# One sum of a seven-product weight scheme moved from VectorE to an accumulating DMA, and steps at five places of a decoder layer moved

## The chip, the core and the metric

The kernel runs on one core of a Trainium2 chip. It is one launch; the time is device microseconds of the program. TensorE (PE) does matmuls and transposes, VectorE (DVE), ScalarE (ACT) and GpSimd (POOL) do the rest, SyncE (SP) and GpSimd issue DMAs. Times of before: 1010.71, 1011.93 and 1009.23 us, median 1010.71.

## The reference, cut to what matters

One decoder layer, batch 1, 256 tokens, width 2048, all in float32. One input projection feeds four causal mixers of 4 heads of 128; each mixer's output is gated, projected, weighted by a sigmoid gate and summed; then the output projection, the residual and a last RMS norm.

```python
h = rms_norm(x, norm_w)
p = h @ w_in                                   # 256 x 2048 times 2048 x N_IN
(z, gate, dsa_qkv, idx_q, idx_k, idx_w, fox_qkv, fox_f, diff_qkv, dil_qkv) = split(p)
branches = (dsa(...), fox(...), diff(...), dilated(...))     # top-k, forgetting, differential, dilated
for b in range(4):
    y = branches[b] * silu(z[b])
    term = sigmoid(gate[b]) * (y @ w_branch[b])
    merged = term if b == 0 else merged + term
return rms_norm(x + merged @ w_out, final_norm_w)
```

In the first mixer an indexer scores all keys for each query (16 small heads) and keeps the best 64, so its attention can start only when that selection is made.

## The kernel before, in words

Every float32 operand is split in two: `hi`, a rounded copy that ACT writes (`split_hi`, line 193), and `lo`, the rest, that DVE writes as raw minus hi (`split_lo`, line 206). A product of one 128-row block is three matmuls (lines 362 to 364: hi with hi, hi with lo, lo with hi).

Most weight columns are done in groups of 1024 output columns by 2048 rows. One half of the rows is done plainly: the four *c* units c2a, c2b, c1a, c1b, of 24 matmuls each. The other half is a 2 by 2 block product done with seven block products instead of eight (`seven`, line 432): units u1 to u7 of 12 matmuls each. They need sums of weight blocks B11, B12, B21, B22, each 128 partitions by 2048 numbers, 1 MB, in raw slots 0, 1, 3 and 2. `plus` (line 173) makes such a sum on DVE in place: B12+=B11 (u5), B12+=B22 (u6), B11=B12-B11 (u7), B21+=B12 (u4). They also need sums of the activations, made once for each source, `asum`, split into the tile `sf` (lines 420 to 429). There are 16 such groups of w_in, four for each branch (qk, zv, and two of the gate, here gate group 1 and 2), and a 17th, the *late* group, for columns of w_out at the end. Products gather in four PSUM banks X, Y, Z, W; between products ACT and DVE read a bank before the next product writes it (lines 526 to 565). Of the `read`s in `seven`, that of u7 is line 530 on ACT, that of Z by c2b lines 534 and 554.

The order is one list of units. For unit i the loop at the end of the program emits `low` (the lo split of the half five halves ahead), `high` (the hi split seven halves ahead; at a unit's second half also the `pre` sums of the unit two further), the unit's matmuls, its `post` reads, perhaps one step of the running threads, then `begin` (the start of new threads). Eight hi and six lo half buffers, shared in turn, hold the splits, so a split waits for the matmuls that used its buffer before. A slot is filled anew when `free` is called on it; SP's queue issues these loads in order. GpSimd's queue issues the DMAs of the merge buffers `md` and `mp`, of bias tables, and of x for the residual.

Everything that is not a weight product is a thread, a generator: the norm of x (`rms_thread`, which writes `rp`), the indexer and top-k with the gate logarithms (`ps_ix`, lines 726 to 750; `cps`, lines 664 to 669; `lf`), heads (`lps`, `ptp`, `o`, and for the differential mixer `od` and `otd`), merges (`mtp`, lines 908 to 921). At each `yield` a thread gives way. A step of all threads is run each time that the costs of the units since the last one reach 20; a product costs 12, any other unit 24. A unit with a `need` first drains the threads that it names.

The loop and the threads' pace:

```python
for h in range(2):
    low(2 * i + h + LO - 1)
    high(2 * i + h + HI - 1)
    u.mm(u, h)
for f in u.post:
    f()
since += u.cost
if since >= PACE:
    since = 0
    run_threads()
begin(u)
```

## Time and profile before

| what | value |
| --- | --- |
| median of three runs | 1010.71 us (1009.23 to 1011.93) |
| profiled execution | 1009.36 us |
| its span | 1007.7 us |
| busy PE, DVE, ACT, POOL | 958.3, 856.1, 630.1, 47.5 us |
| mean granted clock of TensorE | 0.977 |
| DMA | 195.81 MB, mean 194 GB/s |

The span is the time from the first instruction to the last in the profiled execution; the rest of its time lies around it. Busy shares are means over stages: PE is busy 95% of the span, and what is left is seen best in its list of waits. A wait names who waited, for what, and how long. The granted clock is a share of full speed; in a window with a low value every matmul takes longer.

### The profile page before, as it was taken

How to read it: one execution, taken by the hardware profiler on the slowest of the kernel's cores; microseconds unless marked ns; L12 is line 12 of the kernel's file. 1: busy time of each engine (PE TensorE's matmuls, PEld its weight loads, DVE VectorE, ACT ScalarE, POOL GpSimd, SP SyncE). 2: the span in 40 equal slices, each digit the busy share in tenths (PEclk: the TensorE clock that was granted, in tenths of full speed). 3: DMA queues.
4: the chain of work that ended last, by engine and by line, in shares of the span. 5: the costliest groups of instructions: out<-in, count | busy, mean ns of one | idle time of the engine just before them, and what ended most of it. 6: DMA issues, size and time to landing. Idle time of an engine off the chain costs nothing.

```text
span 1007.7 us, 12090 instructions
## 1 busy us (share of the span) xinstructions
PE 958.3 (95%) x4443; PEld 793.4 (79%) x4443; DVE 856.1 (85%) x1016; ACT 630.1 (63%) x809; POOL 47.5 (5%) x67
## 2 busy tenths in 40 slices
PE   9979996999999999999999999979999999985996
PEld 8857885778888888888888877868888888873786
DVE  5689999999898989987997998968898998499762
ACT  5756853697655667974566778745556796353541
POOL 2010000000000000000100000101000000100130
PEclk9999999899999999999999999989999999987999
DMA  9926463455767556468857464648755645931702
GB/s 319 295 90 222 139 212 122 168 167 204 264 220 238 180 170 235 173 201 260 233 173 246 170 202 132 213 164 207 257 182 173 220 174 201 392 135 42 264 29 84
DMA packets 100043, 195.81 MB, mean 194 GB/s; under 512 B 7811, under 2 KB 10021, under 8 KB 99600
## 3 DMA queue, kind: packets, MB, share of 16 engines
q1 hardware_dynamic: 96240, 181.06, 52.8%
q0 software_dynamic: 3712, 13.98, 5.3%
q8 instruction: 35, 0.57, 0.2%
q14 instruction: 24, 0.20, 0.1%
q10 hardware_dynamic: 32, 0.01, 0.0%
HBM read 186.61 MB, written 8.41 MB: 194 GB/s over the span
## 4 chain that ended last, share of the span: by engine, by line
PE 81%; DVE 10%; issue 3%; ACT 3%; DMA 2%; POOL 0%; ACTq 0%; POOLq 0%; DVEq 0%
PE ps_g L362 10%; PE ps_g L363 10%; PE ps_g L364 10%; PE ps_zv L362 5%; PE ps_zv L364 5%; PE ps_zv L363 5%; PE ps_qk L364 5%; PE ps_qk L362 5%; PE ps_qk L363 5%; DVE wlo L206 4%; PE ps_o L363 2%; PE ps_b L362 2%; PE ps_b L363 2%; PE ps_b L364 2%; PE ps_o L362 2%
## 5 line engine op out<-in xcount | busy, mean ns | idle before, releaser
L193 ACT ACTIVATE whi<-raw 128x1024 fp32r<-128x1024 f32 (+1 forms) x439 | 444.6, 1051 | 231.2 <-DVE raw L173 93.3
L206 DVE TENSOR_TENSOR wlo<-raw,whi 128x1024 fp32r<-128x1024 f32 (+1 forms) x439 | 519.0, 1218 | 52.5 <-ACT whi L193 19.1
L173 DVE TENSOR_TENSOR raw<-raw 128x2048 f32<-128x2048 f32 x68 | 155.6, 2288 | 30.8 <-DMA raw<-in_w_in_dram 30.2
L364 PE MATMUL ps_g<-wlo,hT 128*128 128x512 f32 x352 | 137.7, 391 | 8.3 <-DVE wlo L206 8.3
L362 PE MATMUL ps_g<-whi,hT 128*128 128x512 f32 x352 | 138.9, 395 | 1.4 <-ACT g L530 1.4
L363 PE MATMUL ps_g<-whi,hT 128*128 128x512 f32 x352 | 137.3, 390 | 0.0
L364 PEld LDWEIGHTS ps_g<-wlo,hT 128*128 128x128 f32 x352 | 66.3, 188 | 22.7 <-DVE wlo L206 8.7
L362 PEld LDWEIGHTS ps_g<-whi,hT 128*128 128x128 f32 x352 | 66.3, 188 | 15.9 <-ACT g L530 1.8
L363 PEld LDWEIGHTS ps_g<-whi,hT 128*128 128x128 f32 x352 | 66.3, 188 | 13.4
L362 PE MATMUL ps_zv<-whi,hT 128*128 128x512 f32 x176 | 68.9, 391 | 0.0
L364 PE MATMUL ps_zv<-wlo,hT 128*128 128x512 f32 x176 | 68.6, 390 | 0.0
L363 PE MATMUL ps_qk<-whi,hT 128*128 128x512 f32 x176 | 68.5, 389 | 0.0
L363 PE MATMUL ps_zv<-whi,hT 128*128 128x512 f32 x176 | 68.5, 389 | 0.0
L362 PE MATMUL ps_qk<-whi,hT 128*128 128x512 f32 x176 | 68.5, 389 | 0.0
L364 PE MATMUL ps_qk<-wlo,hT 128*128 128x512 f32 x176 | 68.5, 389 | 0.0
L362 PE MATMUL ps_g<-whi,sf 128*128 128x512 f32 x128 | 54.2, 423 | 0.7 <-DVE tok L544 0.7
L362 PE MATMUL ps_b<-whi,yT 128*128 128x512 f32 x128 | 51.7, 404 | 0.0
L363 PE MATMUL ps_b<-whi,yT 128*128 128x512 f32 x128 | 51.2, 400 | 0.0
L364 PE MATMUL ps_b<-wlo,yT 128*128 128x512 f32 x128 | 51.1, 399 | 0.0
L363 PE MATMUL ps_g<-whi,sf 128*128 128x512 f32 x128 | 50.9, 397 | 0.0
L364 PE MATMUL ps_g<-wlo,sf 128*128 128x512 f32 x128 | 50.7, 396 | 0.0
L362 PE MATMUL ps_o<-whi,mT 128*128 128x512 f32 (+1 forms) x112 | 41.3, 369 | 0.0
(265 smaller groups left out, 1527.4 us busy)
## 6 DMA issues: line engine op xcount, KB each, us to landing
raw<-in_w_in_dram SPq DMA_DIRECT2D x132, 1024.0 KB, 5.1
raw<-in_w_branch_dram SPq DMA_DIRECT2D x16, 1024.0 KB, 5.2
raw<-in_w_out_dram SPq DMA_DIRECT2D x16, 1024.0 KB, 5.8
md<-g POOLq DMA_DIRECT2D x12, 512.0 KB, 5.3
raw<-in_w_in_dram SPq DMA_DIRECT2D x7, 512.0 KB, 9.6
xs<-in_x_dram SPq DMA_DIRECT2D x8, 256.0 KB, 8.1
mp<-md POOLq DMA_DIRECT2D x4, 512.0 KB, 3.7
xf<-in_x_dram POOLq DMA_DIRECT2D x2, 1024.0 KB, 10.9
```

Source lines behind the costliest of these rows:

```text
L173: nc.vector.tensor_tensor(to.tile, of.tile, to.tile, op=op)
L193: nc.scalar.activation(u.parts[0][h][:, s_], raw[:, s_], AF.Copy)
L206: nc.vector.tensor_tensor(u.parts[1][h][:, s_], raw[:, s_], u.parts[0][h][:, s_].bitcast(F32), op=ALU.subtract)
L362: nc.tensor.matmul(ps, ahi, u.hi(k)[:, cols], start=first, stop=False, skip_group_check=on)
L363: nc.tensor.matmul(ps, alo, u.hi(k)[:, cols], start=False, stop=False, skip_group_check=on)
L364: nc.tensor.matmul(ps, ahi, u.lo(k)[:, cols], start=False, stop=last, skip_group_check=on)
```

## The change

- In the 16 groups of w_in the DVE sum B11=B12-B11 goes. Instead a DMA issued by GpSimd behind u3's lo split adds B12, read again from HBM, into B22 (`plus_dram`), and u7 is computed with B22. B11's slot is freed at u1, B12's at u2, B22's at u7. u7 stands one place further back, behind u2; the read of bank W moves from u2 to c1a.
- `scaled`, the softmax scaling of heads, moves from DVE to ACT.
- The norm thread has one yield more before `rp`, the differential thread one more before `otd`, the first merge one more before its transposes.
- The units of branch 0's first two groups (qk and zv) cost 24, so that threads run a step at each.
- The late group has the order c2a, c2b, u1, u2, u5, u3, u6, u7, c1a, u4, c1b; u1 and u2 cost 24; two sums move to other places; the last branch unit starts its thread before the step instead of behind it.
- The scratch for GpSimd's DMA descriptors doubles.

```diff
@@ rms_thread
         yield
         yield
+        yield
         rp = att_ps("rp")
@@ seven
-        u1 = unit("P1", B11, product("Y", whole(0, s0), True), [read(ev.p1, "Y")])
+        u1 = unit("P1", B11, product("Y", whole(0, s0), True), [read(ev.p1, "Y")],
+                  frees=[] if late else [B11])
         u3 = unit("P3", B22, product("Z", form(0, 4), not late))
-        u6 = unit("P6", B12, product("Y", form(0, 0)), [read(ev.u2, "Y")],
-                  pre=[lambda: plus(B12, B22), lambda: free([B22])])
-        u7 = unit("P7", B11, product("Y", form(1, 0)), [read(ev.u3, "Y")], frees=[B11],
-                  pre=[lambda: plus(B11, B12, ALU.subtract)])
+        u3.after += [lambda: free([B22])] if late else [lambda: plus_dram(B22, B12)]
+        second = [lambda: plus(B12, B22)]
+        fourth = [lambda: plus(B21, B12), lambda: free([B12])]
+        u6 = unit("P6", B12, product("Y", form(0, 0)), [read(ev.u2, "Y")])
+        u7 = unit("P7", B11 if late else B22, product("Y", form(1, 0)), [read(ev.u3, "Y")],
+                  frees=[B11 if late else B22],
+                  pre=[lambda: plus(B11, B12, ALU.subtract)] if late else [])
         u2 = unit("P2", B21, product("X", whole(0, s0 + 4), True))
-        u2.after += [lambda: plus(B21, B12)] + ([] if late else [lambda: free([B12])])
@@
         if late:
-            u6.after += [lambda: free([B12])]
+            u5.after += second[:1]
+            u6.after += fourth
+            u1.cost = u2.cost = 24
             u7.post += [read(ev.c12, "Z", True), read(ev.c22, "W", True)]
-            return [c2a, c2b, u1, u5, u3, u2, u6, u7, c1a, u4, c1b]
+            return [c2a, c2b, u1, u2, u5, u3, u6, u7, c1a, u4, c1b]
+        u6.pre += second
+        u2.after += fourth
         c2b.post += [read(ev.c12, "Z", True)]
-        u2.post += [read(ev.c22, "W", True)]
-        return [u5, u1, u3, c2a, u6, c2b, u7, u2, c1a, u4, c1b]
+        c1a.post += [read(ev.c22, "W", True)]
+        return [u5, u1, u3, c2a, u6, c2b, u2, u7, c1a, u4, c1b]
@@ scaled
-            nc.vector.tensor_scalar(e[:, SL[t]], e[:, SL[t]], r[:, t:t + 1], None, op0=ALU.mult)
+            nc.scalar.activation(e[:, SL[t]], e[:, SL[t]], AF.Copy, scale=r[:, t:t + 1])
@@ diff_thread
         yield
         yield
+        yield
         ot = att_ps("otd")
@@ merge_thread
         yield
+        if n == 0:
+            yield
@@ branch_units
+        units[0].eager = b == 3 and n == 3
@@ the list of units
+        first = qkvz_units(b, off, scale, att_threads(b, fn))
+        if b == 0:
+            for u in first:
+                u.cost = 24
+        units += first
@@ the loop
+        if u.eager:
+            begin(u)
         since += u.cost
         if since >= PACE:
             since = 0
             run_threads()
-        begin(u)
+        if not u.eager:
+            begin(u)
@@ the launch
-                    dynamic_dma_scratch_size=1024)
+                    dynamic_dma_scratch_size=2048)
```

Lines in the changed kernel stand 1 to 18 further down. PE at the start of the first group, before (`ps_misc` is the small last product of the indexer's inputs, `msT` its result turned, `sf` the activation sums, `hT` the activations; `vps` reads a bias table):

```order
L372 MATMUL ps_misc<-hT,wlo 84x256
L293 MATMUL rp<-dg,ones 128x256
L362 MATMUL ps_qk<-whi,sf 128x512
...
L364 MATMUL ps_qk<-wlo,hT 128x512
L645 MATMUL mtp<-ident,msT 128x84 x2
L314 MATMUL vps<-oh_sb,co_sb 13x383
```

The same place in the changed kernel:

```order
L374 MATMUL ps_misc<-hT,wlo 84x256
L364 MATMUL ps_qk<-whi,sf 128x512
...
L366 MATMUL ps_qk<-wlo,sf 128x512
L295 MATMUL rp<-dg,ones 128x256
L654 MATMUL mtp<-ident,msT 128x84 x2
L316 MATMUL vps<-oh_sb,co_sb 13x383
L364 MATMUL ps_qk<-whi,hT 128x512
```

The product P5 (12 matmuls with sf) now stands ahead of rp, and the transposes of msT follow rp at once; before, P5 and P1 (24 matmuls) stood between rp and them.

ACT in branch 0's first gate group, before, from the read of bank Z behind c2b (line 554) to the one behind u7 (line 530), with steps of heads between (`sz`, `pt`, `lg`):

```order
L554 ACT_TABLE_LOAD
L554 ACTIVATE g<-g 128x512
L593 ACTIVATE sz<-turn 128x512
L790 ACTIVATE pt<-ptp 128x384
L779 ACT_TABLE_LOAD
L779 ACTIVATE lg,sm<-lg,mx 128x128
L779 ACTIVATE lg,sm<-lg,mx 128x256
L193 ACTIVATE whi<-raw 128x1024 x2
L530 ACTIVATE g<-ps_g,rst 128x512
```

The same place in the changed kernel:

```order
L563 ACT_TABLE_LOAD
L563 ACTIVATE g<-g 128x512
L602 ACTIVATE sz<-turn 128x512
L799 ACTIVATE pt<-ptp 128x384
L788 ACT_TABLE_LOAD
L788 ACTIVATE lg,sm<-lg,mx 128x128
L788 ACTIVATE lg,sm<-lg,mx 128x256
L194 ACTIVATE whi<-raw 128x1024 x4
L539 ACTIVATE g<-ps_g,rst 128x512
L602 ACTIVATE sz<-turn 128x512
L804 ACTIVATE lg<-lg,sm 128x128
L804 ACTIVATE lg<-lg,sm 128x256
```

Two more splits stand ahead of the read of u7's bank, and the two scalings of a head (line 804) are new on ACT.

DVE at the end, before, from the last four splits of merged activations (`mT`) to `sf`:

```order
L921 TENSOR_TENSOR mT<-mtp_7305,mT 128x2x256
L921 TENSOR_TENSOR mT<-mtp_7312,mT 128x2x256
L206 TENSOR_TENSOR wlo<-raw,whi 128x1024
L173 TENSOR_TENSOR raw<-raw 128x2048
L206 TENSOR_TENSOR wlo<-raw,whi 128x1024
L1007 TENSOR_TENSOR xf<-xf,ps_o 128x512
L420 TENSOR_TENSOR asum<-mT 128x1024 x2
L423 TENSOR_TENSOR asum<-asum 128x512
L424 TENSOR_TENSOR asum<-asum 128x512
L425 TENSOR_TENSOR asum<-asum 128x512
L426 TENSOR_TENSOR asum<-asum 128x512
L429 TENSOR_TENSOR sf<-asum,sf 128x8x128 x2
```

The same stretch in the changed kernel:

```order
L207 TENSOR_TENSOR wlo<-raw,whi 128x1024 x2
L422 TENSOR_TENSOR asum<-mT 128x1024 x2
L207 TENSOR_TENSOR wlo<-raw,whi 128x1024
L174 TENSOR_TENSOR raw<-raw 128x2048 x2
L207 TENSOR_TENSOR wlo<-raw,whi 128x1024
L1021 TENSOR_TENSOR xf<-xf,ps_o 128x512
L425 TENSOR_TENSOR asum<-asum 128x512
L426 TENSOR_TENSOR asum<-asum 128x512
L427 TENSOR_TENSOR asum<-asum 128x512
L428 TENSOR_TENSOR asum<-asum 128x512
L431 TENSOR_TENSOR sf<-asum,sf 128x8x128 x2
```

The first sums of the merged activations (line 422) now stand ahead of the last splits and weight sums, with the latter two in one place.

## Rows read from the trace of the kernel before

In a row of waits stand the waiting instruction, what it waited for, us in total, times and the longest. In a row of windows stand the stretch, its length, then busy us and instructions of PE, PE's weight load, DVE, ACT and POOL, the granted clock, the share of the DMA engines and GB/s. In a row of the timeline stand start and duration in us, and in brackets the idle time ahead and what ended it.

**Rows 1.** The page, part 1: busy time, share, instructions by engine.

```profile
PE 958.3 (95%) x4443; PEld 793.4 (79%) x4443; DVE 856.1 (85%) x1016; ACT 630.1 (63%) x809; POOL 47.5 (5%) x67
```

**Rows 2.** Waits of PE: waiter, awaited, us in total, times, longest.

```profile
PE ps_o L362 <- ACT sf L428: 11.7, 1, 11.7
PE ps_g L364 <- DVE wlo L206: 8.3, 1, 8.3
PE otd L880 <- DVE on L873: 5.7, 1, 5.7
PE rp L293 <- DVE qf L399: 5.0, 1, 5.0
PE mtp L916 <- DVE g L908: 3.3, 1, 3.3
```

**Rows 3.** Windows around four of the waits: us, busy, PEclk, DMA share, GB/s.

```profile
61.00:67.00 6.00, 1.02 (x6) 0.62 (x5) 5.30 (x6) 4.29 (x8) 0.49 (x1) 0.94 0.19 73
168.00:186.00 18.00, 8.97 (x24) 6.36 (x23) 17.54 (x37) 6.91 (x8) 0.00 (x0) 0.62 0.16 52
663.00:670.00 7.00, 1.27 (x10) 0.99 (x8) 4.67 (x8) 2.44 (x8) 0.88 (x2) 0.78 0.14 50
911.00:930.00 19.00, 6.64 (x18) 4.62 (x17) 17.39 (x16) 4.97 (x6) 0.00 (x0) 0.64 0.17 55
```

**Rows 4.** Windows of the first stage and of the stretch behind it.

```profile
61.00:186.00 125.00, 109.88 (x504) 89.66 (x503) 119.82 (x179) 79.62 (x102) 4.69 (x7) 0.93 0.46 151
186.00:870.00 684.00, 676.86 (x3073) 558.59 (x3072) 604.36 (x689) 462.52 (x590) 19.34 (x28) 1.00 0.62 206
```

**Rows 5.** Lines of DVE: the weight sums; then line 795, min/median/max ns.

```profile
L173 DVE TENSOR_TENSOR raw<-raw 128x2048 f32<-128x2048 f32 x68 | 155.6, 2288 | 30.8 <-DMA raw<-in_w_in_dram 30.2
L795 DVE TENSOR_SCALAR lg<-lg,sm x32: 278/317/352, 194.8 to 839.2; 128x128 f32<-128x128 f32 x16, 128x256 f32<-128x256 f32 x16
```

**Rows 6.** Timeline, start and us: PE and DVE from the first wait on.

```profile
66.70 0.77 PE L293 MATMUL rp<-dg,ones 128*128 128x256 f32 x1 [4.98 <-DVE qf L399]
72.21 0.42 DVE L399 TENSOR_TENSOR msT<-ps_misc,halves 84x256 f32<-84x256 f32 x1
90.54 0.17 DVE L660 SCALAR_TENSOR_TENSOR lf<-fl,fe 128x8 f32<-128x8 f32 x1 [0.71 <-ACT fe L658]
```

**Rows 7.** Timeline, DVE: the weight sum ahead of the third wait.

```profile
662.13 2.29 DVE L173 TENSOR_TENSOR raw<-raw 128x2048 f32<-128x2048 f32 x1 [3.07 <-DMA raw<-in_w_in_dram]
```

**Rows 8.** Timeline, DVE in the last stretch.

```profile
882.75 1.23 DVE L206 TENSOR_TENSOR wlo<-raw,whi 128x1024 fp32r<-128x1024 f32 x1 [8.71 <-ACT whi L193]
922.73 2.36 DVE L429 TENSOR_TENSOR sf<-asum,sf 128x1024 fp32r<-128x1024 f32 x2 [1.12 <-ACT sf L428]
```

**Rows 9.** Timeline, PE: first matmul behind the last wait, two later ones.

```profile
923.70 0.79 PE L362 MATMUL ps_o<-whi,sf 128*128 128x512 f32 x1 [11.71 <-ACT sf L428]
942.00 0.39 PE L362 MATMUL ps_o<-whi,mT 128*128 128x512 f32 x1
943.36 0.39 PE L362 MATMUL ps_o<-whi,mT 128*128 128x512 f32 x1
```

**Rows 10.** Timeline, a gate group: u7's last matmul, its read, PE's wait.

```profile
203.53 0.39 PE L364 MATMUL ps_g<-wlo,sf 128*128 128x512 f32 x1
209.82 0.66 ACT L530 ACTIVATE g<-ps_g,rst 128x512 f32<-128x512 f32 x1
210.54 0.50 PE L362 MATMUL ps_g<-whi,hT 128*128 128x512 f32 x1 [1.41 <-ACT g L530]
```

**Rows 11.** Line 779 on ACT: min/median/max ns.

```profile
L779 ACT ACTIVATE lg<-lg,mx x40: 402/448/497, 190.2 to 832.6; 128x128 f32<-128x128 f32 x20, 128x256 f32<-128x256 f32 x20
```

**Rows 12.** DMA: the software queue; issues, KB each, us to landing.

```profile
q0 software_dynamic: 3712, 13.98, 5.3%
raw<-in_w_in_dram SPq DMA_DIRECT2D x132, 1024.0 KB, 5.1
md<-g POOLq DMA_DIRECT2D x12, 512.0 KB, 5.3
```

More of the change, by code (lines that the diff above doesn't have):

```diff
@@ L96, in __init__ @@
         self.cost = 24
+        self.eager = False
     def hi(self, k):
@@ L938, in ev @@
                     load_m(i)
-        return tok_units(w_branch[b], n * 512, lambda k: (V["yT"][:, k, 0], V["yT"][:, k, 1]),
+        units = tok_units(w_branch[b], n * 512, lambda k: (V["yT"][:, k, 0], V["yT"][:, k, 1]),
                          (0, 2, 4, 5)[n:n + 1], ev,
@@ L942, in branch_units @@
                          start=[(f"merge{n}", lambda: merge_thread(n))] if b == 3 else [])
+        units[0].eager = b == 3 and n == 3
+        return units
     def open_final():
@@ L1086, in body @@
                               (2, O_DIFF, 0.125, diff_thread), (3, O_DIL, HSCALE, head_thread)):
-        units += qkvz_units(b, off, scale, att_threads(b, fn))
+        first = qkvz_units(b, off, scale, att_threads(b, fn))
[3 more added lines that the diff above has]
+        units += first
         for i in range(2):
```

## The prediction, made before the changed kernel was run

> **What bounds the kernel now.** I read the page first. TensorE (PE) is busy 958.3 of 1007.7 us [rows 1], so at most about 49 us are to be won while its matmuls stay as they are. Next the waits of PE: five single ones, 11.7, 8.3, 5.7, 5.0 and 3.3 us, hold 34.0 us of it [rows 2]. They cost more than they last: in the windows around four of them the granted clock is 0.94, 0.62, 0.78 and 0.64 [rows 3], and the first matmul behind the longest takes 0.79 us, where later ones take 0.39 and follow each other every 0.227 us (six between 942.00 and 943.36) [rows 9]. Then windows by stage: between 61 and 186 us DVE is busy 119.8 of 125.0 us and PE 109.9; between 186 and 870 us PE is busy 676.9 of 684 and DVE 604.4 [rows 4]. So the first stage is DVE's, the long middle is PE's, and the end is a chain through DVE, followed below.
>
> **Part by part.** The ledger is made against the profiled execution, 1009.36 us: its span of 1007.7 and 1.66 around it. It lies 1.35 us under the median of 1010.71.
>
> *The 16 accumulating DMAs.* Sixteen weight sums of 2.288 us leave DVE [rows 5], 36.6 us. In the middle DVE has 80 us to spare already, so there this buys PE nothing. In the first stage two of them go before PE is through the first half of the third group, 4.6 us. Each DMA reads 1 MB from HBM and adds it into slot 2. No row shows 1 MB accumulated; the nearest are the plain 1 MB load, 5.1 us to landing, and 512 KB by GpSimd, four plain and eight accumulating, 5.3 us [rows 12]. So 5 to 11 us (twice the latter); I take 9, near the row that accumulates. What hides it: u3's last half is split about three units ahead of PE, u7's first half four, so between them PE runs u5, u1, u3 and half of c2a, 48 matmuls, 10.9 us; and PE itself misses u7 only after the rest of c2a, u6, c2b and u2, 60 matmuls, 13.6 us more. Price zero; without the cover ACT stands still in 16 groups. GpSimd, busy 5% [rows 1], has time to issue them; the merge and bias DMAs queue behind them, and those are used much later than they are asked for.
>
> *Softmax scaling from DVE to ACT.* 32 instructions of 317 ns leave DVE, 10.1 us [rows 5], all behind 194 us, where DVE has room: nothing for PE. ACT gains 32 of the kind of line 779 (same shapes, a per-partition operand), 448 ns [rows 11], 14.3 us over 16 heads. ACT is busy 462.5 of 684 us there [rows 4], but its queue is in order and the reads of PE's banks stand in it. Between 0 and 14; I take +1.
>
> *First stage: the waits for rp (5.0) and behind the top-k burst (8.3).* rp goes behind the first product, which covers its 5.0 us. But the two transposes of msT now follow rp directly, while before a product of 24 matmuls lay between. msT is made at 72.21 for 0.42 us [rows 6], behind the same DVE work. With P5 started where rp stood, PE reaches them at about 67.3 and waits some 5 us: the wait has changed its name. The six cps products move up too, to behind u3; their operand (lf) was ready at 90.54 [rows 6], and though its chain through ACT starts earlier now, I reckon a second wait there, 0 to 4 us. On the credit side the index and top-k steps now run in every unit of branch 0, so the burst in which DVE worked 17.5 of 18 us and PE 9.0 [rows 3] is spread out. What decides is DVE's sum: it is 95.9% busy in this stage, loses 4.6 us and keeps everything else. If its idle time (5.2 us) also vanished, 9.8 us would be won; if the new waits of PE make DVE idle in turn, up to 5 are lost. I take -3: the 4.6, less a bit of new idle.
>
> *The wait for otd (5.7).* One unit more is asked for between the scaling and the transposes, but the last head is drained at once all the same. DVE however stood 3.07 us for a raw load just ahead of it [rows 7]. That slot (B12) is now freed one unit earlier, 12 matmuls or 2.7 us, so the load lands about when DVE asks. The rest of the chain (bank read, ACT, GpSimd's power, DVE) stays. -2.5, between 0 and -5.7.
>
> *The end: the waits for mtp (3.3) and sf (11.7).* DVE stands 8.71 us until a w_out half is split on ACT, then works nearly without a break from 882.75 to the sums that it splits at 922.73 [rows 8]. I counted its rows in both orders over that stretch: 11 halves, 3 weight sums, 4 merges and 8 mT splits, the same. So sf comes about when it did, 1 us earlier as its first sums no longer stand behind the last weight sum. What changes is what PE has done by then: u2 stands ahead of u5, so behind sf there remain u5, u3, u6 and u7 before c1a instead of five products. Before, c1a began at 942.00, 18.3 us behind 923.70 [rows 9]. After: 922.6, four products of 12 matmuls, 10.9 us, and 2.8 for low clock and sums: 936.3, so -5.7. The later yield of the merge moves the 3.3 us into the wait for sf; they are not won a second time. Ends: 0 (a sum for u6 or u7 comes late) and -20 (both waits and their clock).
>
> *u7 directly before c1a.* Before, u2's 12 matmuls lay between u7 and c1a, which writes the same bank Y after six matmuls of its own; ACT must have read the bank by then. In the group shown, u7's last matmul starts at 203.53, ACT reads at 209.82 for 0.66, and PE waits 1.41 us for it [rows 10]. After, 2.7 us of cover go. ACT gains those 2.7 between the reads of c2b and of u7 and does two more splits there, 2.0 us, so its lag shrinks by 0.7 only and the wait grows by 2.0. The other 15 groups show no such wait; each can lose 0 to 2.0, so 2 to 32 us in all. No wait is the nearer row: I take twice the low end, +4.
>
> Sum: -3 -2.5 -5.7 +4 +1 = -6.2; 1003.2 as a profiled execution, and with the 1.35 us to the median about 1004.5 us.
>
> **Rivals.** (1) *The waits really go.* 5.0, 8.3 and 5.7, about 6 of clock behind them, and the 5.7 of the end, less the 5 of bank Y and ACT: -25.7, 985 us; at best 970, if sf's chain falls too. For it: code at every one of the five places is moved. Against it: DVE's sums in the first stage and at the end, which the order leaves nearly whole. (2) *Bank Y holds PE*, the slower side. It decides from the point where ACT's lag behind u7's last matmul exceeds six matmuls and a few short head products, about 2.5 us, and each head gives ACT 0.9 us more. If ten of the sixteen groups, those with heads beside them, lose 2.0 us, 20 go against 11 won: +9, 1019 us. For it: the lag of 6.95 us shown; against: one wait among 16 before. (3) *The accumulating DMA lands late.* Beyond 11 us ACT stands in front of u7's split, with every bank read queued behind it; at 16 us, 5 us in 16 groups, of which PE would feel perhaps a third, +27, less 11: 1027 us. Against: the software queue took 5.3% of the DMA engines for 13.98 MB [rows 12], 3.8 us per MB, so 16.8 MB more ask 64 us of engines that stand free for 38% of the middle [rows 4]. By the Trainium skill ("DMA: Bandwidth & Descriptors", section "Issuing engines are not separate DMA queues") DMAs of all issuing engines run interleaved on the same 16 engines, so these would also slow the weight loads that stand beside them. No run here shows yet by how much; it is why this rival has a chance at all. (4) *Nothing to see*: the first stage finds its waits elsewhere and bank Y takes what the end gives, 1008 to 1013 us.
>
> **How the numbers follow.** What the measurement can tell from no change is about 0.3%, 3 us. My forecast, 996 to 1008, gets 0.47; rival 1 0.14; rival 2 0.14; rival 3 0.05; rival 4 0.20. Faster, under 1007.7, is rival 1 and nearly all of the forecast, 0.59; within, rival 4 and a little of the forecast, 0.21; slower, rivals 2 and 3 with a margin, 0.20. The range leaves out the better half of rival 1 and most of rival 3: 985 to 1018; the forecast's own is 996 to 1008.
>
> **What would show it.** Right: among the waits of PE the one for rp has become one for msT near 70 us, with perhaps one for cps near 85, no stop of 8 us near 168, and a wait of about 7 us for sf near 920; c1a 13 to 14 us behind that; DVE's busy time near 810 us, ACT's near 645; no wait of ACT on the accumulated slot. Wrong: many waits of PE on ACT's read of bank Y (rival 2); ACT standing for the DMA in front of u7's split in each group (rival 3); no wait of PE over 3 us and a granted clock near 1.00 throughout (rival 1); or the msT and cps waits together longer than those for rp and the burst were, which would turn my -3 into a loss.

## The result, and the profile after

The changed kernel takes 1019.87 us (median of three runs, 1018.99 to 1021.1) against 1010.71: a ratio of 1.0093 with a 95% interval of 1.0065 to 1.012. It is 9.2 us slower. The forecast was 1004.5 us, 6.2 us faster, with a range to 1018.

Where the time went is read first from when PE comes to the same work in both profiled executions. Three matmuls of before (start, duration): the first of branch 0's output product, the first of the last branch's, and the last of all.

```profile
268.13 0.39 PE L362 MATMUL ps_b<-whi,yT 128*128 128x512 f32 x1
866.57 0.39 PE L362 MATMUL ps_b<-whi,yT 128*128 128x512 f32 x1
999.63 0.28 PE L364 MATMUL ps_o<-kept,mT 128*128 128x256 f32 x1
```

The same three after:

```profile
270.15 0.39 PE L364 MATMUL ps_b<-whi,yT 128*128 128x512 f32 x1
872.86 0.39 PE L364 MATMUL ps_b<-whi,yT 128*128 128x512 f32 x1
1009.27 0.28 PE L366 MATMUL ps_o<-kept,mT 128*128 128x256 f32 x1
```

So 2.0 us are lost in the first stage, 4.3 in the middle and 3.3 at the end, 9.6 in all, and the profiled executions differ by as much (1018.99 - 1009.36). The page's first part (compare [rows 1]) has DVE busy 36.5 us less and ACT 12.6 more; PE's list of instructions is as long as it was.

```profile
PE 964.6 (95%) x4443; PEld 795.8 (78%) x4443; DVE 819.6 (81%) x968; ACT 642.7 (63%) x841; POOL 72.7 (7%) x83
```

By their rows the 16 sums took 36.6 us of DVE before and the scalings 10.2, and both are gone, so 46.8 had been meant to go; the lo splits of 128 by 1024 now occupy DVE for 521.0 us instead of 516.3, at the same mean of 1.22 us each, and where the rest lies is open. PE is busy 6.3 us more for as many instructions, and idle 3.3 us more (52.7 of its span against 49.4). So by the profile's busy time two thirds of the loss are matmuls that took longer, and only one third is waiting.

The waits of PE after (waiter, awaited, us, times, longest), to be held against [rows 2]:

```profile
PE ps_o L364 <- ACT sf L430: 7.9, 1, 7.9
PE otd L890 <- DVE on L882: 5.5, 1, 5.5
PE mtp L654 <- DVE msT L401: 5.3, 1, 5.3
PE ps_qk L364 <- ACT tok L539: 4.3, 2, 2.6
PE ps_o L364 <- DVE xf L1023: 3.6, 1, 3.6
PE ps_o L365 <- DVE mT L933: 3.3, 1, 3.3
PE ps_zv L364 <- DVE v L535: 3.0, 1, 3.0
PE cps L673 <- DVE lf L669: 2.3, 1, 2.3
```

The five waits before had 34.0 us; these eight have 35.2. The stop of 8.3 us behind the top-k burst is gone and so is the wait for rp, but in their place stand msT, cps and v. The wait for sf is 3.8 us shorter, and xf (3.6) is new. The wait for otd is as it was. New too is `tok`, twice: PE waits for ACT's read of u7's bank in two qk groups.

The windows of the first stage and of the stretch behind it, as [rows 4]:

```profile
61.00:188.00 127.00, 112.48 (x499) 90.22 (x498) 115.56 (x177) 81.02 (x101) 8.64 (x10) 0.92 0.58 171
188.00:872.00 684.00, 673.63 (x3058) 555.13 (x3057) 568.86 (x640) 471.59 (x620) 39.93 (x41) 1.00 0.73 224
```

DVE's sum in the first stage fell by 4.3 us, but in a window 2 us longer: its idle time went from 5.2 to 11.4 us. For PE the stretches between the same two matmuls say more, first the first stage up to branch 0's output product, then the end from the last branch's product to the first matmul of c1a, each before and after:

```profile
61.00:268.13 207.13, 190.60 (x875) 156.52 (x874) 195.02 (x281) 141.77 (x185) 4.69 (x7) 0.96 0.53 177
61.00:270.15 209.15, 194.08 (x874) 157.85 (x873) 185.14 (x269) 147.32 (x193) 9.92 (x11) 0.95 0.64 195
866.57:942.00 75.43, 58.89 (x249) 47.60 (x248) 60.87 (x60) 30.63 (x35) 1.06 (x2) 0.86 0.48 177
872.86:951.63 78.77, 61.44 (x250) 49.10 (x249) 60.72 (x60) 30.26 (x35) 1.06 (x2) 0.85 0.49 180
```

In the first stage PE's idle time is 1.5 us shorter after, but its matmuls take 3.5 us longer. At the end they take 2.6 us longer, with 0.8 us more idle time. In the middle it is the other way: 0.2 us of matmuls and 4.1 us of idle time. Between 188 and 872 us the DMA engines' share rose from 0.62 to 0.73. The software queue and the accumulating loads in the page's DMA part (queue: packets, MB, share; issues, KB, median us to landing):

```profile
q0 software_dynamic: 12160, 30.76, 15.0%
raw<-in_w_in_dram POOLq DMA_DIRECT2D x16, 1024.0 KB, 9.6
```

### The profile page after: what moved, and what is told of

It reads as the page before. It is cut to its first block, busy times and chain, and to the rows that moved or that the text cites. A ratio compares the mean times of both kernels' runs of the same rounds, so it can differ in the third digit from the quotient of the medians.

```text
span 1017.3 us, 12138 instructions
## 1 busy us (share of the span) xinstructions
PE 964.6 (95%) x4443; PEld 795.8 (78%) x4443; DVE 819.6 (81%) x968; ACT 642.7 (63%) x841; POOL 72.7 (7%) x83
## 3 DMA queue, kind: packets, MB, share of 16 engines
q1 hardware_dynamic: 96240, 181.06, 51.8%
## 5 line engine op out<-in xcount | busy, mean ns | idle before, releaser
L174 DVE TENSOR_TENSOR raw<-raw 128x2048 f32<-128x2048 f32 x52 | 119.0, 2289 | 13.5 <-DMA raw<-in_w_in_dram 12.9
L364 PE MATMUL ps_qk<-whi,hT 128*128 128x512 f32 x176 | 70.4, 400 | 4.3 <-ACT tok L539 4.3
L365 PE MATMUL ps_qk<-whi,hT 128*128 128x512 f32 x176 | 70.0, 398 | 0.0
L178 POOL DMA_DIRECT2D raw<-in_w_in_dram x16 | 21.7, 1357 | 448.0 <-DVE wlo L207 432.5
L364 PE MATMUL ps_g<-whi,sf 128*128 128x512 f32 x128 | 52.2, 408 | 0.0
L365 PE MATMUL ps_g<-whi,sf 128*128 128x512 f32 x128 | 49.9, 390 | 0.0
```

The lines of the kernel that those rows point to most:

```text
L174: nc.vector.tensor_tensor(to.tile, of.tile, to.tile, op=op)
L178: nc.gpsimd.dma_start(to.tile.rearrange("p (k n) -> p k n", k=of.nk), of.src[of.k0 * P:(of.k0 + of.nk) * P, of.c0:of.c0 + of.n] .rearrange ...
L364: nc.tensor.matmul(ps, ahi, u.hi(k)[:, cols], start=first, stop=False, skip_group_check=on)
L365: nc.tensor.matmul(ps, alo, u.hi(k)[:, cols], start=False, stop=False, skip_group_check=on)
```

## The experiments

Ratios are against runs of the kernel before on the same chip, with their 95% intervals.

### The accumulating DMA in two groups: the bias load later

Of the 16 accumulating DMAs two land far later than the others. The first of them, after: GpSimd's issues around it, then ACT and PE (start, duration, in brackets the idle time ahead and its releaser).

```profile
488.01 0.86 POOL L946 DMA_DIRECT2D md<-g  x1 [4.87 <-DVE g L944]
488.55 1.12 POOL L306 DMA_DIRECT2D bias<-vdr  x1
489.33 1.66 POOL L178 DMA_DIRECT2D raw<-in_w_in_dram  x1
...
506.70 7.70 ACT L194 ACTIVATE whi<-raw 128x1024 fp32r<-128x1024 f32 x8 [11.02 <-DMA raw<-in_w_in_dram]
517.08 0.67 ACT L539 ACTIVATE tok<-ps_qk,rst 128x512 f32<-128x512 f32 x1
...
517.80 0.50 PE L364 MATMUL ps_qk<-whi,hT 128*128 128x512 f32 x1 [2.59 <-ACT tok L539]
```

In the first group of a branch the last merge sum of the branch ahead (512 KB, accumulating) and the bias table (512 KB) are issued just ahead of the sum of 1 MB. It lands 17.3 us behind its issue. ACT stands 11.02 us in front of the split, then works through eight splits without a break, stands 1.71 us for a sum of DVE and does a ninth, and the read of u7's bank behind them is late: PE waits 2.59 us. At 728.42 the same happens again with 1.70. The edit asks for the bias tables of branches 2 and 3 some units later, behind the sum:

```diff
-            units[-1].post.append(lambda b=b: new_bias(4 * b))
+            later.append((len(units) + 8, b))
+    for i, b in later:
+        units[i].post.append(lambda b=b: new_bias(4 * b))
```

> The changed kernel, but the 512 KB bias load of branches 2 and 3 is asked for nine units later, so it no longer stands ahead of the accumulating DMA in GpSimd's queue. Theory A (the late accumulating DMA, 17.3 and 16.4 us to landing in the qk groups of branches 2 and 3, holds ACT 11.0 and 10.1 us, then the read of u7's bank, then PE): both landings fall to 9 to 11 us, ACT's two waits to under 5 us, the two waits of PE on line 539 in qk (4.3 us) go, and the time falls by 4 to 5.5 us against the changed kernel. Theory B (bank Y is late because ACT carries more work and u7 stands next to c1a, whatever the DMA does): the DMA lands earlier, the two waits stay over 1 us each, and the time moves by less than 1.5 us.

Measured 1015.41 us, 1.005 (1.0035 to 1.0066): 4.5 us less than the change. The gain of 0.43% is more than the half-widths of the two intervals make together (0.32%, as the root of the sum of their squares). In its trace the sum goes first:

```profile
489.90 0.86 POOL L946 DMA_DIRECT2D md<-g  x1 [4.86 <-DVE g L944]
491.03 1.33 POOL L178 DMA_DIRECT2D raw<-in_w_in_dram  x1 [0.27 <-issue]
491.79 1.35 POOL L306 DMA_DIRECT2D bias<-vdr  x1
...
515.77 0.69 ACT L539 ACTIVATE tok<-ps_qk,rst 128x512 f32<-128x512 f32 x1 [0.48 <-PE ps_qk L366]
```

ACT now reads the bank 0.48 us after PE has written it, and PE waits in neither group. The landing times of the 16 sums (min, median, max) show the queue, of the change and then of this kernel:

```profile
DMA to landing us min/median/max: 8.5/9.6/17.3
```

```profile
DMA to landing us min/median/max: 8.5/9.6/12.5
```

From branch 0's product to the last branch's it takes 599.0 us in this trace, against 602.7 in the change and 598.4 before. What follows: most of the loss in the middle, 3.7 of 4.3 us, is the order of three transfers in GpSimd's queue, not a general lateness. Less came than was expected of the sum itself: its landing fell to 12.5 us and not to 9 to 11, and ACT still stands 6.1 us for it, which no longer reaches PE.

### The late group as before

The late group's order, sums and costs, the merge's yield and the early start go back.

```diff
...
-            u5.after += second[:1]
-            u6.after += fourth
-            u1.cost = u2.cost = 24
-            return [c2a, c2b, u1, u2, u5, u3, u6, u7, c1a, u4, c1b]
+            u6.after += [lambda: free([B12])]
+            return [c2a, c2b, u1, u5, u3, u2, u6, u7, c1a, u4, c1b]
...
-        if n == 0:
-            yield
...
```

> The changed kernel with the late group as it was before (order of its units, its sums, costs of 12, no extra yield in the first merge, the last merge begun as before). Theory A (the late part of the change costs time: sf comes 2.2 us later since DVE must wait for merge products that PE now delivers in pairs, and u7 then waits for DVE's read of u6): the time falls by 3 to 4 us, and the stretch from the first product of the last branch unit group to the end is as long as before, 133.4 us against 136.7. Theory B (the end is late because the loads of w_out land later beside more traffic): the stretch stays over 136 us, and the time moves by less than 1 us.

Measured 1016.49 us, 1.0059 (1.0041 to 1.0078), 3.4 us less than the change. The gain of 0.34% only just exceeds what the two intervals make together (0.33%); the trace bears it out. From the last branch's first product to the last matmul of all it takes 131.9 us, against 136.4 in the change and 133.1 before. In all seven traces with the end of before it takes 131.9 to 133.4 us, in the four with the new one 134.1 to 136.4 (those with slots changed in the last branch left aside). The parts of the loss stand in the trace of the change. DVE (the restart, a pair of mT splits, sf, and the splits ahead of the read of u6), then PE at the first matmul with sf, at u7's first and at c1a's first:

```profile
889.42 1.23 DVE L207 TENSOR_TENSOR wlo<-raw,whi 128x1024 fp32r<-128x1024 f32 x1 [9.09 <-ACT whi L194]
913.20 2.48 DVE L933 TENSOR_TENSOR mT<-mtp,mT 128x512 fp32r<-128x512 f32 x4 [2.97 <-ACT mT L932]
931.64 2.36 DVE L431 TENSOR_TENSOR sf<-asum,sf 128x1024 fp32r<-128x1024 f32 x2 [1.12 <-ACT sf L430]
941.86 4.62 DVE L207 TENSOR_TENSOR wlo<-raw,whi 128x1024 fp32r<-128x1024 f32 x4
946.40 0.68 DVE L1023 TENSOR_TENSOR xf<-xf,ps_o 128x512 f32<-128x512 f32 x1
...
932.60 0.80 PE L364 MATMUL ps_o<-whi,sf 128*128 128x512 f32 x1 [7.87 <-ACT sf L430]
947.22 0.77 PE L364 MATMUL ps_o<-whi,sf 128*128 128x512 f32 x1 [3.59 <-DVE xf L1023]
951.63 0.40 PE L364 MATMUL ps_o<-whi,mT 128*128 128x512 f32 x1
```

From DVE's restart to sf it is 42.2 us, against 40.0 in [rows 8]: DVE stands 2.97 us for the merged activations. From the first matmul with sf to c1a it is 19.0 us, against 18.3 in [rows 9], although a product of 12 fewer lies between. The four splits of 4.62 us stand in DVE's queue ahead of the read of u6, and u7 writes that bank next: 3.59 us of wait. Behind this stand PE's granted clock is 0.61 over u7, nearer the lower of its two levels (1.2 and 2.4 GHz) than the upper (window, its length, busy times, granted clock, DMA share, GB/s):

```profile
947.20:951.60 4.40, 4.38 (x12) 3.55 (x13) 2.23 (x2) 0.00 (x0) 0.00 (x0) 0.61 1.03 359
```

u7's 12 matmuls took 4.4 us there, and 2.7 at the pace of [rows 9]: 1.7 us more.

### The start as before

```diff
-        yield
         rp = att_ps("rp")
...
-        if b == 0:
-            for u in first:
-                u.cost = 24
```

> The changed kernel with the first stage's order as before: rp ahead of the first product, branch 0's qk and zv products at cost 12. The two or three weight sums that the accumulating DMA takes off DVE stay gone. Theory A (DVE's sum decides the stage and the moved steps only make DVE idle, 11.4 us against 5.2): the first branch product, at 270.2 us in the changed kernel and 268.1 before, comes at 262 to 265, and the time falls by 5 to 8 us. Theory B (the stage is not bound by DVE's sum, the removed sums bring nothing): it comes at 268, the time falls by 2 us.

Measured 1017.42 us, 1.0079 (1.0062 to 1.0096). The difference of 0.14% is less than the two intervals make together (0.32%), and PE comes to branch 0's output product at 270.24 us, where it came at 270.15 in the change: the new start is not shown to cost or to bring anything.

### The sum on DVE instead of by DMA

```diff
-        u3.after += [lambda: free([B22])] if late else [lambda: plus_dram(B22, B12)]
+        u3.after += [lambda: free([B22])] if late else [lambda: plus(B22, B12)]
```

> The changed kernel, in its order, with a DVE addition into slot 2 in place of each of the 16 accumulating DMAs (it adds the block as it stands in the slot by then, so this one value differs). Theory A (the DMA's late landing costs the two waits of PE in the qk groups of branches 2 and 3): those waits go, 4 to 5 us; the first stage gets two or three sums of 2.3 us back on DVE and loses 3 to 7 us; the sum over the run is between -2 and +3 us. Theory B (the order alone makes bank Y late): the two waits stay, and the time rises by 3 to 7 us.

This adds B12 as its slot holds it by then, so the values differ, but the work is of the same size. Measured 1018.2 us, 1.0081 (1.0067 to 1.0096). Both waits for `tok` are gone, as theory had it: from branch 0's product to the last branch's it takes 598.0 us, 4.7 less than in the change, a second sign that the DMA is what the middle lost by. But PE comes to branch 0's output product 8.9 us late instead of 2.0. The sums stand on DVE again there, as they do in the kernel before, though at other places of its queue and with the new start. How much is the place and how much the start is open. The two effects nearly cancel in the time.

### Three edits undone at once, and msT's transposes later

The first kernel has the edits of the first three experiments together. What is left of the change is the sum by DMA with u7 behind u2, the scaling on ACT and the yield ahead of otd.

> Bias loads later, late group as before and first stage's order as before, all three together; what is left of the change is the accumulating DMA with u7 behind u2, the scaling on ACT and the yield before otd. If the three costs are separate, their gains add: 4.5, 3.4 and 2.4 us of 1019.9, so 1009 to 1011 us, no longer to be told from the kernel before. If they overlap (the same loss seen three times), it stays at 1013 us or more.

Measured 1011.21 us, 1.001 (1.0002 to 1.0019). The three ratios undone singly take 0.43, 0.34 and 0.14% off the change; together 0.83%. So nearly all of the loss is found, and with the start and the end as before, 36.6 us less of DVE's sums for 16 MB added by DMA are worth nothing to PE.

Why its first stage gains nothing either, with the old start and less on DVE, shows in its waits of PE:

```profile
PE rp L294 <- DVE qf L400: 5.0, 1, 5.0
PE ps_g L365 <- DVE wlo L207: 4.3, 1, 4.3
PE ps_qk L363 <- ACT tok L540: 4.1, 1, 4.1
```

The top-k stop of 8.3 us has fallen to 4.3, by about the sums that went, and 4.1 us of wait for ACT's read of u7's bank have come in the first group. The next section puts u2 between u7 and c1a again: this wait falls to 1.2 there.

The second kernel keeps the new start, the late group as before and the bias later, and gives the thread of msT two yields at its start.

```diff
     def misc_thread():
+        yield
+        yield
```

> Bias loads later and late group as before; the first stage in the changed order, but with the transposes of msT (and with them cps and the index steps) two units later, behind u3. Theory A (the stage loses by the early waits for msT and cps and by the low clock that follows them, not by DVE's sum): both waits go or fall under 1.5 us, the granted clock between 66 and 90 us is above 0.9, and the time falls by 4 to 8 us against 1012 us, which the first two edits alone should give. Theory B (DVE's sum and the top-k rounds decide, wherever PE waits): the same time is lost later, at the bank reads near 160 to 180 us, and the time is 1010 to 1013 us.

Measured 1012.56 us, 1.0017 (1.0009 to 1.0026). The wait for msT is gone, and two others have grown:

```profile
PE ps_zv L364 <- ACT v L541: 7.5, 1, 7.5
...
PE cps L677 <- DVE lf L673: 4.9, 1, 4.9
```

12.4 us where the change had 10.6 (msT, v and cps). The second theory had this: the order moves the place of the wait in the first stage, and its sum stays.

### u7 ahead of u2 again, and the scaling on DVE again

Both start from the kernel with three edits undone.

```diff
-        c1a.post += [read(ev.c22, "W", True)]
-        return [u5, u1, u3, c2a, u6, c2b, u2, u7, c1a, u4, c1b]
+        u2.post += [read(ev.c22, "W", True)]
+        return [u5, u1, u3, c2a, u6, c2b, u7, u2, c1a, u4, c1b]
```

> As the run with the three parts undone, but u7 stands ahead of u2 again, so that u2's 12 matmuls lie between u7 and c1a; the accumulating DMA stays. Theory A (u7 next to c1a makes PE wait for ACT's read of bank Y, 4.4 us in branch 0's first group when the first stage has its old order): that wait falls under 1.5 us and the time falls by 3 to 5 us against that run. Theory B (the DMA, now asked for by ACT one unit earlier, holds ACT in more groups): waits of ACT on the accumulated slot rise above 40 us in sum, waits of PE on line 539 appear in other groups, and the time rises.

Measured 1021.9 us, 1.0116 (1.0102 to 1.013): 10.7 us more. ACT stands for a load 15 times, 14 of them for an accumulated slot, each in another group (67.2 us; in the kernel it started from 8 times, 28.7 us). The row of ACT's waits:

```profile
ACT whi L194 <- DMA raw<-in_w_in_dram: 67.6, 15, 9.4
```

PE's wait for u7's bank in the first group fell from 4.1 to 1.2 us, as the first theory had it, but the stop behind the top-k burst grew from 4.3 to 9.5 and the wait for otd from 5.6 to 7.4. So with the DMA, u7's place one further back costs something at the bank and gains more by giving the transfer its time.

```diff
-            nc.scalar.activation(e[:, SL[t]], e[:, SL[t]], AF.Copy, scale=r[:, t:t + 1])
+            nc.vector.tensor_scalar(e[:, SL[t]], e[:, SL[t]], r[:, t:t + 1], None, op0=ALU.mult)
```

> As the run with the three parts undone, but the softmax scaling back on DVE. Theory A (the scaling on ACT is hidden): within 1 us of that run. Theory B (ACT's queue makes bank reads late in the heads): 1 to 3 us less, with fewer waits of PE on bank reads between 188 and 870 us.

Measured 1012.11 us, 1.0017 (1.0008 to 1.0026) against 1.001 (1.0002 to 1.0019) without the edit. No difference is seen: the scaling is hidden on either engine.

### Which load DVE waits for: the slots of w_branch

The waits for otd and, by way of mtp and sf, the end follow a stand of DVE for a load, 3.07 us in [rows 7] and 8.71 in [rows 8]; after, 2.95 and 9.09. The awaited slots are held until then by blocks of w_branch, which line 940 of the kernel before puts into slots 0, 2, 4 and 5. Two kernels change those numbers in the kernel before, with nothing of the change: one in branches 0 to 2, one in branch 3.

```diff
-                         (0, 2, 4, 5)[n:n + 1], ev,
+                         ((2, 4, 3, 5) if b < 3 else (0, 2, 4, 5))[n:n + 1], ev,
```

> The kernel before, with one edit: the four w_branch blocks of branches 0 to 2 go through raw slots 2, 4, 3, 5 instead of 0, 2, 4, 5. Theory A (DVE's 3 us wait for a load ahead of the drain before otd is a wait for B11 in slot 0, which the first w_branch block holds, and not for B12 as the prediction had it): B11 is asked for as soon as the gate group is done with it, DVE's waits on loads (30.2 us, 15 times) fall under 10 us, PE's wait for otd falls from 5.7 to 2.5 to 4 us, and the time falls by 2 to 4 us. Theory B (slot 0 is not what holds the load): the wait for otd and the time stay within 1 us.

Measured 1006.12 us, 0.9965 (0.9953 to 0.9977). DVE's weight sum ahead of the otd wait no longer stands for its load, and the wait for otd falls from 5.7 to 2.6 us. DVE's waits for loads fell less than expected, from 30.2 us in 15 to 21.7 in 12, where under 10 had been forecast. A row of the timeline, then one of PE's waits:

```profile
661.30 2.28 DVE L173 TENSOR_TENSOR raw<-raw 128x2048 f32<-128x2048 f32 x1
```

```profile
PE otd L880 <- DVE on L873: 2.6, 1, 2.6
```

```diff
-                         (0, 2, 4, 5)[n:n + 1], ev,
+                         ((0, 2, 4, 5) if b < 3 else (0, 2, 1, 3))[n:n + 1], ev,
```

> The kernel before, with one edit: the four w_branch blocks of the last branch go through raw slots 0, 2, 1, 3, so that slots 4 and 5 are free for the first two w_out blocks. Theory A (the chain to sf starts 8.7 us late since c2a's block waits for slot 4, which a w_branch block holds, and then lands in the crowd of the last big transfers): the w_out block is there before DVE asks, PE's waits for mtp and sf (3.3 and 11.7 us) fall together by 6 to 10 us, and the time falls by 6 to 10 us. Theory B (DVE's work alone sets sf): DVE gets ahead on c2a but stands elsewhere, and the time moves by less than 2 us.

Measured 1004.51 us, 0.9939 (0.9928 to 0.9951). DVE's stand at the restart is 0.95 us instead of 8.71, the wait for mtp falls from 3.3 to 0.5, that for sf stays, though a fall of 6 to 10 us had been expected of the two together:

```profile
876.16 1.23 DVE L206 TENSOR_TENSOR wlo<-raw,whi 128x1024 fp32r<-128x1024 f32 x1 [0.95 <-issue]
...
919.42 0.80 PE L362 MATMUL ps_o<-whi,sf 128*128 128x512 f32 x1 [11.90 <-ACT sf L428]
```

DVE's row of [rows 8] stands 6.6 us earlier here. The first matmul with sf comes 51.7 us behind the first of the last branch's product (867.74 here), where before it was 57.1: the stretch is 5.4 us shorter. Of these 2.6 are idle time of PE and 2.8 are matmuls that took less: between 884 and 905 us the granted clock is 1.00, where it was 0.84. What is left in front of sf is DVE's work, but for 2.16 us of standing for one more load.

### Both slot edits, with and without parts of the change

Four kernels carry both slot edits: on the three edits undone, on the change with the bias later, on the kernel before, and on the change with the bias later and the late group as before.

> As the run with the three parts undone (the accumulating DMA stays), plus both slot edits: w_branch through slots 2, 4, 3, 5 and at the end 0, 2, 1, 3. If both slot theories hold and are separate from the change, 1011.2 less 2 to 4 and 6 to 10: 997 to 1003 us. If the 16 MB of accumulating traffic is in the way of the earlier loads: 1004 us or more, with waits of ACT on the accumulated slot above the 30.4 us of that run.

> The changed kernel with the bias loads later, plus both slot edits. The late order of the change (u2 ahead of u5, merge products in pairs) was 3.4 us worse than the old one while DVE started late. If the late load was why (DVE short of time), the changed order now ends no later than the old: 1015.4 less 8 to 12, 1003 to 1007 us. If the order itself is worse (the read of u6 behind four splits on DVE): still 3 us over the run with the old order, so 1006 us or more, and a wait of PE for the read of u6 of 3 us or more.

> The kernel before with both slot edits and nothing of the change. Theory A (the accumulating DMA and the scaling on ACT buy PE nothing: DVE's room in the middle is idle, and in the first stage a late read of bank Y takes what the shorter top-k stop gives): as fast as the run that has both slot edits and the DMA, 1001.3 us, within 1.5 us; the two single edits multiply to 0.9904 of before, 1000.3 us. Theory B (36.6 us less on DVE are worth something once the loads come in time): 1003 to 1006 us.

> The changed kernel with the bias loads later, both slot edits and the late group as before; against the run with the changed late group and the same edits, 1002.7 us. Theory A (the changed late order lost 3.4 us only as DVE started it late): the two are within 1.5 us. Theory B (the order itself costs it, by merge products in pairs and by the read of u6 behind four splits): 2.5 to 4 us less than 1002.7.

| kernel with both slot edits | median us | ratio |
| --- | --- | --- |
| kernel before, nothing of the change | 1000.13 | 0.9896 (0.9884 to 0.9909) |
| three edits undone | 1001.28 | 0.991 (0.9897 to 0.9922) |
| change, bias later, late group as before | 1001.95 | 0.9913 (0.99 to 0.9927) |
| change, bias later | 1002.69 | 0.9924 (0.9912 to 0.9937) |

The kernel before with two tuples of slot numbers changed has the lowest median, 10.7 us under it on the same chip; the next two are not told apart from it by their intervals. The two gains multiply (0.9965 times 0.9939 is 0.9904). Nothing of the change is shown to improve it. Its waits of PE:

```profile
PE ps_o L362 <- ACT sf L428: 11.7, 1, 11.7
PE ps_g L364 <- DVE wlo L206: 8.2, 1, 8.2
PE rp L293 <- DVE qf L399: 5.0, 1, 5.0
PE otd L880 <- DVE on L873: 2.6, 1, 2.6
```

Of the kernels with the slots, the one with the new late order and the one with the old differ by 0.7 us, within their intervals: once the load comes early, the order of the late group is not shown to matter to the time. The wait for xf in the new order stays even so, at 3.0 us, as had been expected if the order itself brings it.

## Why the prediction was wrong

**The end (forecast -5.7, measured +3.3).** The step that failed is "sf comes about when it did, 1 us earlier", together with four products and 2.8 us from there to c1a. I counted DVE's rows and found the same work, which was right. But the count holds only while DVE has something to do: with the new order it stood 2.97 us for merged activations, so from its restart sf came 2.2 us later. The 10.9 and 2.8 us to c1a were right as far as they go; 3.59 us of wait and 1.7 of low clock stood in addition (13.7 + 5.3 = 19.0). The bound I gave for a loss was a late sum for u6 or u7. The wait that came was for a bank. In both orders u7 stands right behind u6 and writes the same bank, so DVE must read it between them. Before, u2's 12 matmuls stood ahead of u6 and gave DVE 2.7 us more for its queue: the read started at 938.33, as u6's last matmul (937.90 for 0.39) ended. After, with u2 gone from there, PE was done with u6 at 943.63 and the read started at 946.40, behind the splits. So the 2.7 us of u2 came back as wait, and 1.7 of low clock on top. A larger sum at the end lay elsewhere, in the slot held by w_branch (5.4 us), and I had its row in hand: the stand of 8.71 us in [rows 8]. I read it as the start of the chain and did not ask what held the load.

**The accumulating DMA (forecast 0, measured +4.3 in the middle, nearly all of it by this).** The size was right: 9 us forecast, 9.6 median. The step that failed is "the merge and bias DMAs queue behind them": in two groups the sum queues behind them. I looked at who waits for the merge and bias DMAs, and not at what stands ahead of the sum in the same queue. The cover was also smaller than I said. ACT asked for the slot about 6.4 us behind the issue (in the group at 490, 495.68 against 489.33), since it splits ahead of need; the 10.9 us were counted from PE. That cost ACT 33.1 us in seven waits, and PE waited behind it only in those two groups. Rival 3 had the mechanism right, in 2 groups instead of 16, and I gave it 0.05.

On the queue, the Trainium skill ("DMA: Bandwidth & Descriptors", section "Two DMAs through the same engine are not ordered") says that descriptors of one queue of a DMA engine start in order, though pipelined. The 17.3 and 12.5 us of the two orders agree. Its fit for GpSimd's DMAs (same page, section "Anatomy of one DMA — SWDGE (gpsimd) path"), 2.0 us and the bytes over 436e3, would make an estimated 4.4 us for 1 MB; the accumulating one took 9.6, and the measurement decides.

**otd (forecast -2.5, measured about 0).** The step that failed is "That slot (B12) is now freed one unit earlier" and so "the load lands about when DVE asks". After the change DVE stood 2.95 us in the same place. The sum reads two blocks, B12 in slot 1 and B11 in slot 0, and only slot 0 is one that w_branch holds, by its first block until that block's product is done. With that block in slot 2 the stand was gone and the wait fell from 5.7 to 2.6.

**The first stage (forecast -3, measured +2.0).** msT's wait was forecast at some 5 us near 70 and came to 5.3 at 72.6; cps at 0 to 4, and 2.3 came; the stop near 168 went, as said; DVE's sum fell by 4.3 of 4.6. What failed is "less a bit of new idle": DVE's idle time rose by 6.2 us, above the 5 I allowed. A term was missing as well. I wrote that waits cost more than they last, yet gave the new waits no clock: between 61 and 80 us the granted clock fell from 0.91 to 0.74, between 80 and 100 from 1.00 to 0.91, and only between 160 and 190 did it rise, from 0.77 to 0.91. That PE's matmuls took 3.5 us longer here goes with it; that this is also what left DVE idle is likely, but no run tried it. The size of the loss is open: in the kernel with slots changed only in branch 3, whose program up to here is that of before, the same product began at 269.29, 1.2 us later than before's 268.13, and two kernels that are alike up to here, those from before with the slots changed in the middle and with both, gave 270.45 and 268.18. The 2.0 us lie within such scatter, and neither the old start nor the moved transposes gave a difference outside the intervals. The gain of 3 us did not come in any trace with the new start: there the product began between 270.15 and 272.04, and at 276.99 with the sums on DVE.

**Bank Y (forecast +4).** In the group of [rows 10] the wait fell to 0.55 us. In another group, of zv, ACT's read cost 1.1 us; more was not found outside the two groups with the late DMA. Rival 2 gave nearly the measured time (1019), but by ten groups of 2.0 us where there were four with 6.0 in all, two of them by the DMA: its nearness is luck. The step that failed is that ACT's "lag shrinks by 0.7 only". In this group it shrank from 6.95 us to 3.4 (u7's last matmul at 209.12, the read done at 212.50): before, ACT had stood 4.03 us for DVE's weight sum ahead of this stretch, and after, with the sum of u7 gone from DVE, such stands of ACT took 28.5 us of the whole run instead of 93.3. This is read from the traces, not tried.

**Scaling on ACT (forecast +1).** Not seen; right in size.

**As a ledger.** Forecast: -3 for the first stage, +2.5 for the middle (-2.5 + 4 + 1), -5.7 for the end. Measured: +2.0, +4.3, +3.3. Of the 15.8 us between them 9.0 are the end's, 5.0 the first stage's, 1.8 the middle's, where two errors (bank Y and the DMA) hid each other. Rival 1 fell everywhere: the waits that went were replaced, at 35.2 us against 34.0. The stated range ended at 1018, below the 1019 of rival 2, to which I had given 0.14; that was an error of its own. Of the signs, DVE's busy time near 810 us failed too: 819.6.

## What to carry to other kernels

Where an engine stands for a load, ask first which work holds the slot and whether another free slot would do: two tuples of slot numbers gave 1%, where moving work between engines and places gave nothing that these runs show. A DMA that is put on a queue is priced with what is already in that queue at its tightest place, and its cover is counted from the engine that asks first, here ACT, not from PE. A product that is moved away leaves the other engines less time in the stretch that it leaves, so list what they must get done there before PE's next write, the reads of banks too.

## What the runs showed of the hardware

An accumulating DMA of 1 MB takes 8.5 us at least and 9.6 in the median, against 5.2 for a plain load by SP. In all 16.8 MB of it raised the software queue's share from 5.3% of 1007.7 us to 15.0% of 1017.3, 99 us more of all 16 engines, 5.9 us per MB; I had used 3.8 from the queue's mix before, and the plain loads of the hardware queue take 2.9 (51.8% for 181.06 MB). Yet the plain 1 MB loads beside them landed in 5.2 us as before (5.1): no slowing of the weight loads is seen. In the one queue of GpSimd a transfer's landing depends on what was issued just ahead: 1 MB came 17.3 us after its issue behind a 512 KB accumulating and a 512 KB bias transfer, 12.5 at most without the bias transfer ahead.
